# Layer 0 expert rows: latent rows normalised on TensorE and written plainly, context rows by accumulating DMA

## The chip, the cores and the metric

The kernel runs on one core of a Trainium2 chip. The metric is the device time of one execution in microseconds. Three executions of the kernel before took 1258.33, 1256.99 and 1256.77 us, with a median of 1256.99 us.

## The reference, cut to what matters

Two layers run over 256 latent tokens (x) and 256 context tokens (ctx), each row 1024 wide. After the mixer of a layer, every token row is normalised and modulated, and the 512 rows of layer 0 go through a mixture of 16 experts:

```python
m  = (silu(c) @ mod_w[l] + mod_b[l]).reshape(bsz, 1, 6, D)      # latent rows
mc = (silu(c_ctx) @ mod_w[l] + mod_b[l]).reshape(1, 1, 6, D)    # context rows
...
x = x + m[:, :, 2] * y
h = rms_norm(x, norm2_g[l]) * (1 + m[:, :, 4]) + m[:, :, 3]
if need_ctx:                                                    # layer 0 only
    xc = xc + mc[:, :, 2] * yc
    hc = rms_norm(xc, norm2_g[l]) * (1 + mc[:, :, 4]) + mc[:, :, 3]
    tokens = concatenate([h, hc])                               # 512 rows
    out = hierarchical_moe(tokens, router_g, router_e, w1, w3, w2)
```

With A2 = norm2_g * (1 + m4) and shift = m3, a row is h = rstd * (x * A2) + shift. The rstd is known only when the whole row of x is there; the shift is one row of 1024 numbers for all latent tokens and another for all context tokens. The experts pick their tokens by top-1 group and top-2 experts, so each expert needs a gather of rows of h.

## The kernel before, in words

All is written in one class, `Trunk`, for a scheduler that gives each engine one list of instructions and the semaphore waits between the lists; an engine works off its list in order. Work that may lie beside other work (modulation, shared norms, weight splitting) is written as generators that are woven into the main loops. SBUF is held by an allocator, `Arena` (`F.get`, `F.free`): a tile takes a free block, so what a write has to wait for depends on which block it was given and who used that block last. Weights come through `Stream` objects: `ws` holds loads of 1 MB each, all issued on the SP queue at L159, and `ws.add(F.fits(2048) - n)` gives it all the slots that still fit less a reserve. The reserve for the experts of a layer is the table `RES`.

The modulation rows are made half by half in `mod_half`: 8 k-steps of matmuls (L417), a bias add (L422, L424), a transpose, and four small DMAs on the ACT queue (L439) that write the rows to a DRAM tile `md[l, g]`. `mod_row` (L469) reads such a row back, broadcast over 128 partitions, also on the ACT queue.

`finish` closes the mixer. It loads A2 (`mod_row`), and while the output projection comes out piece by piece (L331 to L333, L550, L553) it makes x * A2 (L1300) into `H`, squares (L1329) and router logits (L1308 to L1323). In layer 0 it makes a DRAM tile `hd` of 512 rows and fills it with the shift rows by four broadcast DMAs from `md` (L1289), two of latent and two of context rows.

`moe` then computes rstd (ends in L298), and in layer 0 scales the four 128-row pieces of `H` by it on ScalarE (L1391) and adds each to `hd` with an accumulating DMA on the POOL queue (L1392). Beside this VectorE works the top-k and the ranks of the tokens (L1422 to L1479). At L1829 and L1835 every engine loads a flag and branches (whether an expert has overflowed). The experts follow: POOL gathers 128 rows of `hd` for each (L1483), TensorE transposes them (L1530), and ScalarE and VectorE split weights and rows for three-term products (L322, L325, L331 to L333, L1539, L1540).

Layer 1 has only latent rows; its rows for the experts don't pass through `hd`. There the same `finish` loads A2 (L469), which L1300 needs.

Of the kernel before, what the change touches and what calls it, by code (L numbers as in the profile page):

```python
# [8 lines left out]
F32 = mybir.dt.float32  # L9
F32R = mybir.dt.float32r  # L10
BF = mybir.dt.bfloat16
I32 = mybir.dt.int32
AF = mybir.ActivationFunctionType
OP = mybir.AluOpType
AX = mybir.AxisListType

P = 128
D = 1024
# [216 lines left out]
BQ = "sync"  # L235
HR = 4
HP = 0, 1, 0, 0
RES = 3, 3
FA = 2, 2
FB = 9, 9  # L240
NYY = 4
# [10 lines left out]
class Trunk:  # L252
# [146 lines left out]
    def mod_half(self, l, g, h):  # L399

        nc, I, F = self.nc, self.I, self.F
        ms, mb = F.get(256), F.get(256)

        def rows(dst, src):
            for i in range(src.shape[0]):
                nc.sync.dma_start(dst[32 * i:32 * i + 32], src[i:i + 1].to_broadcast([32, 256]))
        rows(mb, I["modb"][l, g, h])
        if g == 2:  # L410
            g2 = F.get(256)
            rows(g2[0:64], I["n2g"][l, h])
        acc = self.bank("m")
        for k in range(KC):
            raw = self.wm.take()
            for i in range(4):
                nc.tensor.matmul(acc[32 * i:32 * i + 32, 0:256], self.cs[:, k, :], raw[:, i * 256:(i + 1) * 256],  # L417
                                 start=(k == 0), stop=(k == KC - 1))
            self.wm.done(raw)
            if k < KC - 1:  # L420
                yield
        nc.vector.tensor_tensor(ms, acc[:, 0:256], mb, op=OP.add)  # L422
        if g == 2:
            nc.vector.scalar_tensor_tensor(ms[0:64], ms[0:64], 1.0, g2[0:64], op0=OP.add, op1=OP.mult)  # L424
            F.free(g2)
        F.free(mb)
        if g:
            yield

            tp, dst = self.bank(), (self.sh if g == 1 else self.a2)[l]  # L430
            for b in range(2):
                nc.tensor.transpose(tp[:, b * P:(b + 1) * P], ms[:, b * P:(b + 1) * P], self.ident)
            src = tp[:, 0:256].rearrange("p (b j q x) -> p j q b x", b=2, j=2, q=2)
            for s in range(2):
                nc.vector.tensor_copy(dst[:, s, 4 * h:4 * h + 4].rearrange("p (q b) -> p q b", q=2),
                                      src[:, 2 - g, :, :, s])
        if g:
            for i in range(4):
                nc.scalar.dma_start(self.md[l, g][:, h, i // 2, 256 * (i % 2):256 * (i % 2) + 256],  # L439
                                    ms[32 * i:32 * i + 2])  # L440
            F.free(ms)
        else:
            self.mr[l, h] = ms
        yield
# [811 lines left out]
    def finish(self, l, mix):  # L1256

        F, nc = self.F, self.nc
        ns = len(self.X)
        A2 = F.get(ns, D)  # L1260
        for s in range(ns):
            self.mod_row(A2[:, s], l, 4, s)

        rts, bR = F.get(ns, KC, 32), F.get(ns, 32)
        self.bR = bR
        for s in range(ns):
            nc.vector.tensor_tensor(rts[:, s], self.rt,
                                    self.a2[l][:, s].rearrange("p (k o) -> p k o", o=1).to_broadcast([P, KC, 32]), op=OP.mult)

        pr, pq = F.get(ns, KC, 32), F.get(ns, 32)  # L1270
        for s in range(ns):
            nc.gpsimd.tensor_tensor(pr[:, s], self.rt,
                                    self.sh[l][:, s].rearrange("p (k o) -> p k o", o=1).to_broadcast([P, KC, 32]), op=OP.mult)
            nc.vector.tensor_reduce(pq[:, s], pr[:, s].rearrange("p k c -> p c k"), AX.X, OP.add)
        ps = self.bank()
        nc.tensor.matmul(ps[:, 0:32 * ns], self.msk("ones"), pq.rearrange("p s c -> p (s c)"), start=True, stop=True)
        nc.scalar.copy(bR, ps[:, 0:32 * ns].rearrange("p (s c) -> p s c", s=ns))
        F.free(pr, pq)
        self.ss, junk = F.get(4, 2), F.get(512, dt=BF)

        hb = F.get(2, 3, D, dt=BF) if ns == 1 else None
        if ns == 2:

            H, self.hd = [F.get(2, D) for s in range(2)], self.dp.tile([4 * P, D], F32, name=f"hd{l}")
            for s in range(2):
                src = self.md[l, 1][s, :, 1].rearrange("(o h) c -> o h c", o=1)
                for i in range(2):
                    t = 2 * s + i
                    nc.scalar.dma_start(self.hd[t * P:(t + 1) * P, :].rearrange("p (h c) -> p h c", h=2),  # L1289
                                        src.to_broadcast([P, 2, 512]))  # L1290
        self.ws.add(F.fits(2048) - FA[l])

        lg, hfR = [self.bank("m"), self.bank("a")][0:ns], Ring(F, 2, 2, 256)
        hR = Ring(F, HR, 2, 256) if ns == 1 else None
        wait, kept = ([], [], [], []), {}

        def scaled(c, s):
            sl = slice(256 * c, 256 * c + 256)
            h = kept[c, s] = hR() if ns == 1 else H[s][:, :, sl]
            nc.vector.tensor_tensor(h, self.X[s][:, :, sl], A2[:, s, sl].rearrange("p (o c) -> p o c", o=1)  # L1300
                                    .to_broadcast([P, 2, 256]), op=OP.mult)

        def keep(c, s):
            sl, h = slice(256 * c, 256 * c + 256), kept.pop((c, s))
            if ns == 2:
                return
            for i in range(3):
                nc.scalar.copy(hb[:, :, i, sl], h)  # L1308
                if i < 2:
                    (nc.gpsimd if HP[c] else nc.vector).tensor_tensor(h, h, hb[:, :, i, sl], op=OP.subtract)  # L1310

        def logits(c, s):

            ps, hf = self.bank(), hfR()
            for kk in range(2):
                for i in range(2):
                    nc.tensor.transpose(ps[:, 256 * kk + i * P:256 * kk + (i + 1) * P],
                                        self.X[s][:, i, 256 * c + kk * P:256 * c + (kk + 1) * P], self.ident)
            nc.scalar.copy(hf, ps.rearrange("p (k t) -> p k t", k=2))
            for kk in range(2):  # L1320
                k = 2 * c + kk
                j = k % 4
                nc.tensor.matmul(lg[s][32 * j:32 * j + 32, 0:256], rts[:, s, k], hf[:, kk], start=(k < 4), stop=(k >= 4))  # L1323

        def squares(c, s):
            if c % 2:
                for i in range(2):
                    t = 2 * s + i
                    nc.scalar.activation(junk, self.X[s][:, i, 256 * c - 256:256 * c + 256], AF.Square,  # L1329
                                         accum_out=self.ss[:, t, c // 2:c // 2 + 1])  # L1330

        def last(c, s):
            for i, f in enumerate((scaled, squares, logits, keep)):
                wait[i].append((c, s))
                if len(wait[i]) > LAG[i] * ns:
                    f(*wait[i].pop(0))

        self.pool_share = 0
        run_all(self.out_half(l, 1, mix, ns, last))
        for i, f in enumerate((scaled, squares, logits, keep)):  # L1340
            for cs in wait[i]:
                f(*cs)
        F.free(*self.gates, junk, hfR, *([hR] if hR else []), rts, self.rt, A2)
        self.R.free(*mix)
        if ns == 2:
            self.xgR = Ring(F, 3, D)
            for x in self.xgR.bufs:
                nc.gpsimd.memset(x, 0.0)
        self.ws.add(max(0, F.fits(2048) - FB[l]))
        if l:  # L1350
            self.swap()
        for t in range(2 * ns):
            self.dbg(f"xm{l}_{t}", self.x(t))
        self.moe(l, H if ns == 2 else hb, lg)
# [14 lines left out]
    def moe(self, l, hd, lg):  # L1369
# [15 lines left out]
            stt(L[:, t], lp[:, 32 * t:32 * t + 32], rs[:, t:t + 1], self.bR[:, t // 2], op0=OP.mult, op1=OP.add)  # L1385
        if ns == 2:

            H, hd = hd, self.hd
            for t in range(nt):
                h = H[t // 2][:, t % 2]  # L1390
                nc.scalar.activation(h, h, AF.Copy, scale=rs[:, t:t + 1])  # L1391
                nc.gpsimd.dma_start(hd[t * P:(t + 1) * P, :], h, accum_op=OP.add)  # L1392
            F.free(*H)
        tmp = []

        def T(n):
# [511 lines left out]
    def run(self, stages):  # L1908
        nc, tc, I, F, R = self.nc, self.tc, self.I, self.F, self.R
        w, m = self.sources(stages)  # L1910
        self.ws, self.wm = Stream(nc, F, w, 2048), Stream(nc, F, m, 1024)
        self.md = {(l, g): self.dp.tile([2, 2, 2, 512], F32, name=f"md{l}{g}") for l in range(2) for g in (1, 2)}
        self.mr, self.sh, self.a2 = {}, [F.get(2, KC) for l in range(2)], [F.get(2, KC) for l in range(2)]
        self.rest = self.mods((1, 1), (1, 2)) if "l1" in stages else iter(())
# [135 lines left out]
```

## Time and profile before

| what | value |
|---|---|
| median of three executions | 1256.99 us |
| the profiled execution's own time | 1263.97 us |
| its span | 1262.2 us |
| mean granted TensorE clock | 0.951 |
| TensorE busy | 1109.3 us, 88% |
| VectorE busy | 806.6 us, 64% |
| ScalarE busy | 560.0 us, 44% |
| GpSimd busy | 340.6 us, 27% |
| bytes moved by DMA | 317.09 MB, mean 251 GB/s |

The profile is of one execution, 6.98 us longer than the median of the three. The busy shares are means over stages that have different limits: the experts of layer 0 run from about 376 to 700 us of the span, those of layer 1 from about 1000 us to the end. What follows reads the stages one by one, by waits and by windows.

### The profile page before, as it was taken

To read this page: it belongs to the slowest core of one execution; us is meant where nothing else is said; L and a number is where in the kernel's file an instruction comes from. 1 tells how busy PE (TensorE), PEld (TensorE's weight loads), DVE (VectorE), ACT (ScalarE), POOL (GpSimd) and SP (SyncE) were. 2 spreads that over 40 slices of the span, in tenths; PEclk is the share of its full clock that TensorE was granted. 3 is DMA by queue.
4 is the path that set the end of the run, shared out by engine and by line. 5 is a ranking of instruction groups with operands and counts; after the bars stand their busy time and mean duration, and the time that the engine had idled before them with its cause. 6 is when DMAs were issued, how large, how long until landed. Compare 5 with 4: busy or idle time off the path is not lost. (4 is left out here: it accounts for less than half of the span.)

```text
span 1262.2 us, 18733 instructions
## 1 busy us (share of the span) xinstructions
PE 1109.3 (88%) x7206; PEld 780.4 (62%) x7206; DVE 806.6 (64%) x1376; ACT 560.0 (44%) x893; POOL 340.6 (27%) x214
## 2 busy tenths in 40 slices
PE   3998899999919999999999779988998599999996
PEld 1656665666717777777777356655777365555553
DVE  3576836555639999999898646998387533333232
ACT  3355525333417787887886323343353311111111
POOL 1331422233213444444532211344423200000000
PEclk9998988899959999999999888999998899999999
DMA  9663568266386999999983154343476789999960
GB/s 355 215 207 124 172 191 278 71 239 242 114 238 241 352 353 346 364 362 358 356 312 118 71 143 179 117 134 107 149 273 249 282 315 422 424 423 424 416 277 35
DMA packets 74977, 317.09 MB, mean 251 GB/s; under 512 B 20074, under 2 KB 26314, under 8 KB 46080
## 3 DMA queue, kind: packets, MB, share of 16 engines
q1 hardware_dynamic: 54656, 294.10, 61.4%
q0 software_dynamic: 4896, 10.20, 3.6%
q10 hardware_dynamic: 15328, 11.50, 3.3%
q8 instruction: 60, 0.98, 0.3%
q14 instruction: 37, 0.30, 0.1%
HBM read 310.74 MB, written 14.76 MB: 258 GB/s over the span
## 5 line engine op out<-in xcount | busy, mean ns | idle before, releaser
L322 ACT CAST arena_rw<-arena_f 128x1024 fp32r<-128x1024 f32 x256 | 265.1, 1050 | 177.7 <-PE b L333 111.3
L325 DVE TENSOR_TENSOR arena_rw<-arena_f,arena_rw 128x1024 fp32r<-128x1024 f32 x198 | 260.4, 1357 | 81.5 <-ACT arena_rw L322 80.9
L331 PE MATMUL b<-arena_rw,arena_rr 128*128 128x512 f32 (+1 forms) x736 | 275.1, 375 | 2.7 <-ACT arena_rr L1214 1.2
L332 PE MATMUL b<-arena_rw,arena_rr 128*128 128x512 f32 (+1 forms) x736 | 272.0, 370 | 0.0
L333 PE MATMUL b<-arena_rw,arena_rr 128*128 128x512 f32 (+1 forms) x736 | 270.1, 369 | 0.5 <-DVE arena_rr L1215 0.5
L325 POOL TENSOR_TENSOR arena_rw<-arena_f,arena_rw 128x1024 fp32r<-128x1024 f32 x58 | 144.4, 2490 | 235.8 <-ACT arena_rw L322 220.6
L331 PEld LDWEIGHTS b<-arena_rw,arena_rr 128*128 128x128 f32 x736 | 140.5, 191 | 37.9 <-issue 10.6
L333 PEld LDWEIGHTS b<-arena_rw,arena_rr 128*128 128x128 f32 x736 | 140.0, 191 | 25.6 <-issue 3.3
L332 PEld LDWEIGHTS b<-arena_rw,arena_rr 128*128 128x128 f32 x736 | 140.7, 191 | 21.2 <-issue 1.3
L417 PE MATMUL b<-arena_f,cs 128*32 128x256 f32 x768 | 70.2, 420 | 22.2 <-DMA arena_f<-in_modw 22.0
L331 PE MATMUL b<-arena_rr,arena_rw 128*128 128x512 f32 (+1 forms) x192 | 74.4, 391 | 2.7 <-ACT arena_rw L322 1.4
L1728 PE MATMUL b<-arena_f 128*64 128x256 f32 x656 | 76.0, 381 | 0.0
L333 PE MATMUL b<-arena_rr,arena_rw 128*128 128x512 f32 (+1 forms) x192 | 72.3, 380 | 4.1 <-DVE arena_rw L325 4.1
L332 PE MATMUL b<-arena_rr,arena_rw 128*128 128x512 f32 (+1 forms) x192 | 73.6, 384 | 1.0 <-POOL arena_rr L507 1.0
L1728 PEld LDWEIGHTS b<-arena_f 128*64 128x64 f32 x656 | 46.5, 137 | 24.2 <-issue 2.3
L417 PEld LDWEIGHTS b<-arena_f,cs 128*32 128x32 f32 x768 | 20.8, 113 | 56.3 <-issue 26.8
L1761 ACT CAST arena_rr<-arena_f 64x512 fp32r<-64x512 f32 x32 | 19.8, 618 | 69.7 <-DVE arena_f L1758 69.3
L1733 ACT ACTIVATE arena_f<-b 128x256 f32<-128x256 f32 x16 | 6.2, 385 | 98.0 <-PE b L1728 98.0
L331 PEld LDWEIGHTS b<-arena_rr,arena_rw 128*128 128x128 f32 x192 | 36.7, 192 | 18.2 <-issue 7.4
L1744 DVE COPY arena_f<-b 128x256 f32<-128x256 f32 x16 | 6.8, 424 | 64.1 <-PE b L1742 64.0
L1488 POOL DMA_INDIRECT yd<-arena_f x14 | 33.5, 2390 | 50.5 <-ACT arena_f L1578 50.5
L553 POOL TENSOR_TENSOR arena_f<-arena_f 128x512 f32<-128x512 f32 x21 | 30.5, 1458 | 57.1 <-DVE arena_f L550 54.8
(386 smaller groups left out, 1798.2 us busy)
## 6 DMA issues: line engine op xcount, KB each, us to landing
arena_f<-in_moe SPq DMA_DIRECT2D x192, 1024.0 KB
arena_f<-in_modw SPq DMA_DIRECT2D x96, 512.0 KB
arena_f<-in_wod SPq DMA_DIRECT2D x18, 1024.0 KB
arena_f<-in_wev SPq DMA_DIRECT2D x14, 1024.0 KB
arena_f<-md ACTq DMA_DIRECT2D x8, 512.0 KB
arena_f<-in_tok SPq DMA_DIRECT2D x4, 512.0 KB
yd<-arena_f SPq DMA_DIRECT2D x4, 512.0 KB
hd<-md ACTq DMA_DIRECT2D x4, 512.0 KB
```

The lines of the kernel that those rows point to most:

```text
L322: nc.scalar.copy(h, raw)
L325: eng.tensor_tensor(l, raw, h.bitcast(F32), op=OP.subtract)
L331: nc.tensor.matmul(ps, ah, bh, start=first, stop=False)
L332: nc.tensor.matmul(ps, ah, bl, start=False, stop=False)
L333: nc.tensor.matmul(ps, al, bh, start=False, stop=last)
L417: nc.tensor.matmul(acc[32 * i:32 * i + 32, 0:256], self.cs[:, k, :], raw[:, i * 256:(i + 1) * 256], start=(k == 0), stop=(k == KC - 1))
L553: (nc.vector if last and c == 3 else nc.gpsimd).tensor_tensor(xs, xs, tmp, op=OP.add)
L1488: self.nc.gpsimd.indirect_dma_start(out=yd[:, :], out_offset=bass.IndirectOffsetOnAxis(ap=dst, axis=0), in_=y, in_offset=None, bounds_chec ...
L1728: nc.tensor.matmul(p[64 * c:64 * c + 64, 256 * w:256 * w + 256], x[:, 4 * b + k], raw[:, 512 * k + 256 * c:512 * k + 256 * c + 256], start ...
L1733: nc.scalar.activation(u, p[:, 0:256], AF.Tanh, scale=0.5)
L1744: nc.vector.tensor_copy(ut, ps[:, 0:256].rearrange("p (b c) -> p b c", b=2))
L1761: nc.scalar.copy(yh[r, c], y[r])
```

## The change

In `mod_half` the first two modulation rows of the second group of layer 0 (the shift rows) are also split into three bf16 parts, which four small DMAs on the ACT queue write to a new DRAM tile `mb2`. In `finish` of layer 0, `hd` gets its broadcast fill for the context rows only; the three parts of the latent shift are loaded into a small tile `S3` of 3 partitions. In `moe` the two context pieces are scaled on ScalarE and added to `hd` by POOL's accumulating DMA, as before. For the two latent pieces TensorE multiplies a diagonal matrix of the rstd (`dgR`, made by ScalarE) by x * A2, and a second matmul with ones over 3 partitions adds the shift parts in the same PSUM bank; ScalarE copies the bank back to `H`, and the SP queue writes the rows to `hd` with a plain DMA. The reserve of weight slots for layer 0 goes from 3 to 2.

```diff
-RES = 3, 3
+RES = 2, 3
@@ mod_half
+            if (l, g) == (0, 1):
+                pt = F.get(3, 256, dt=BF)
+                for i in range(3):
+                    nc.vector.tensor_copy(pt[64:, i], ms[64:])
+                    if i < 2:
+                        nc.vector.tensor_tensor(ms[64:], ms[64:], pt[64:, i], op=OP.subtract)
+                for q in range(2):
+                    nc.scalar.dma_start(self.mb2[:, :, h, 256 * q:256 * q + 256], pt[64 + 32 * q:66 + 32 * q])
+                F.free(pt)
@@ finish
-            for s in range(2):
-                src = self.md[l, 1][s, :, 1].rearrange("(o h) c -> o h c", o=1)
-                for i in range(2):
-                    t = 2 * s + i
-                    nc.scalar.dma_start(self.hd[t * P:(t + 1) * P, :].rearrange("p (h c) -> p h c", h=2),
-                                        src.to_broadcast([P, 2, 512]))
+            self.S3 = F.get(D, dt=BF)
+            nc.scalar.dma_start(self.S3[0:3], self.mb2[0].rearrange("i h c -> i (h c)"))
+            src = self.md[l, 1][1, :, 1].rearrange("(o h) c -> o h c", o=1)
+            for t in range(2, 4):
+                nc.scalar.dma_start(self.hd[t * P:(t + 1) * P, :].rearrange("p (h c) -> p h c", h=2),
+                                    src.to_broadcast([P, 2, 512]))
@@ moe
-            H, hd = hd, self.hd
-            for t in range(nt):
-                h = H[t // 2][:, t % 2]
-                nc.scalar.activation(h, h, AF.Copy, scale=rs[:, t:t + 1])
-                nc.gpsimd.dma_start(hd[t * P:(t + 1) * P, :], h, accum_op=OP.add)
-            F.free(*H)
+            H, hd, dgR = hd, self.hd, F.get(2, P)
+            for t in range(2):
+                nc.scalar.activation(dgR[:, t], self.ident, AF.Copy, scale=rs[:, t:t + 1])
+            for t in range(2):
+                h, g = H[0][:, t], H[1][:, t]
+                nc.scalar.activation(g, g, AF.Copy, scale=rs[:, 2 + t:3 + t])
+                nc.gpsimd.dma_start(hd[(2 + t) * P:(3 + t) * P, :], g, accum_op=OP.add)
+                for c in range(2):
+                    sl, ps = slice(512 * c, 512 * c + 512), self.bank("a")
+                    nc.tensor.matmul(ps, dgR[:, t], h[:, sl], start=True, stop=False)
+                    nc.tensor.matmul(ps, self.oneb[0:3], self.S3[0:3, sl], start=False, stop=True)
+                    nc.scalar.copy(h[:, sl], ps)
+                nc.sync.dma_start(hd[t * P:(t + 1) * P, :], h)
+            F.free(*H, self.S3, dgR)
@@ allocation at the start
+        self.mb2 = self.dp.tile([2, 3, 2, 512], BF, name="mb2")
```

New lines stand at other numbers: L1391 and L1392 become L1404 and L1405, L469 becomes L479, L1483 becomes L1502, L1835 becomes L1854, L1300 becomes L1310. The new ones are L445 and L447 (parts on VectorE), L449 (their DMAs), L1401 (diagonal), L1408 and L1409 (the two matmuls), L1410 (copy) and L1411 (plain write).

ScalarE at the start of the experts of layer 0, before; L1391 scales a piece of `H`, L1422 and L1427 are exponentials of the routing, L469 loads a gate row:

```order
L1391 ACTIVATE arena_f<-arena_f 128x1024 [waits DMAHW3_49,DVE_49]
L1391 ACTIVATE arena_f<-arena_f 128x1024 [waits DMAHW4_49]
L1391 ACTIVATE arena_f<-arena_f 128x1024 x2
L1422 ACTIVATE arena_f<-arena_f 128x16 [waits DVE_49,Activation_49]
L1427 ACTIVATE arena_f<-arena_f 128x4 [waits DVE_49]
L469 DMA arena_f<-md_73 128x2x512 [waits DMAHW7_49,DVE_49,Activation_49]
L1829 TENSOR_LOAD arena_f [waits DMAHW1_49,DVE_49]
```

The same place of ScalarE in the changed kernel (L1441 and L1446 are the two exponentials):

```order
L1401 ACTIVATE arena_f<-mskt,arena_f 128x128 [waits DMAHW6_49,DVE_49,Activation_49]
L1401 ACTIVATE arena_f<-mskt,arena_f 128x128
L1404 ACTIVATE arena_f<-arena_f 128x1024
L1410 COPY arena_f<-b_2550 128x512 [waits PE_49]
L1404 ACTIVATE arena_f<-arena_f 128x1024
L1410 COPY arena_f<-b_2554 128x512 [waits PE_49]
L1441 ACTIVATE arena_f<-arena_f 128x16 [waits DMAHW4_49,DVE_49]
L1410 COPY arena_f<-b_2561 128x512 [waits PE_49]
L1446 ACTIVATE arena_f<-arena_f 128x4 [waits DVE_49]
L1410 COPY arena_f<-b_2565 128x512 [waits DMAHW7_49,PE_49]
```

Two scalings are replaced by four copies that wait for TensorE, the exponentials now stand between these copies, and the gate row's load has moved behind the branch.

SP and POOL at the same place in the changed kernel; first SP, where L1411 writes latent rows to `hd` (before, the row ahead of TENSOR_LOAD was another weight load, and no weight load stood between TENSOR_LOAD and the branch):

```order
L159 DMA arena_f<-in_moe 128x2048 [waits DMAHW5_49,DMAHW0_49,DVE_49]
L1411 DMA hd_2203<-arena_f 128x1024 [waits DMAHW1_49,Activation_49]
L1411 DMA hd_2203<-arena_f 128x1024 [waits DMAHW2_49,Activation_49]
L1848 TENSOR_LOAD arena_f [waits DMAHW6_49,DVE_49]
L1848 ISA x2
L159 DMA arena_f<-in_moe 128x2048 [waits DMAHW2_49,DMAHW3_49,DMAHW1_49,DVE_49]
L1854 COMPARE_AND_BRANCH
```

Then POOL, where the first gather stands ahead of the branch (before, it stood behind it and behind four accumulating DMAs):

```order
L1405 DMA hd_2203<-arena_f 128x1024 [waits DMAHW2_49,DVE_49,Activation_49]
L1405 DMA hd_2203<-arena_f 128x1024 [waits Activation_49]
L1502 DMA arena_f<-hd_2203,arena_f 128x1024 [waits DMASW1_49,DMAHW1_49,DMASW0_49,DMAHW2_49,DVE_49,Pool_49]
L1848 TENSOR_LOAD arena_f [waits DMAHW6_49,DVE_49]
L1854 COMPARE_AND_BRANCH
```

The gather now waits for two semaphores of POOL's own queue and two of the hardware queues, and SP holds a weight load in front of its branch that waits for hardware DMAs.

ScalarE's queue in layer 1, around the load of A2, before; `md_75` is the modulation row, L439 writes it, L469 loads it, L1214 copies transposed rows of the mixer's output out of PSUM:

```order
L439 DMA md_75<-arena_f 2x256 [waits DMAHW4_49]
L322 CAST arena_rw<-arena_f 128x1024 [waits PE_49]
L322 CAST arena_rw<-arena_f_6980 128x1024 [waits DMAHW6_49,PE_49]
L322 CAST arena_rw<-arena_f_6980 128x1024 [waits PE_49]
L1214 ACTIVATE arena_rr_6976<-b_7333,cst 128x128 [waits PE_49]
L1214 ACTIVATE arena_rr_6976<-b_7346,cst 128x128 [waits PE_49]
L1277 COPY arena_f<-b_7363 128x32 [waits PE_49]
L1214 ACTIVATE arena_rr_6976<-b_7333,cst 128x128 [waits DVE_49]
L469 DMA arena_f<-md_75 128x2x512 [waits DMAHW4_49,DMAHW3_49,DMAHW7_49,DMAHW0_49,Pool_49]
```

The same place in the changed kernel:

```order
L439 DMA md_76<-arena_f 2x256 [waits DMAHW1_49]
L322 CAST arena_rw<-arena_f 128x1024 [waits PE_49]
L479 DMA arena_f<-md_76 128x2x512 [waits DMAHW3_49,DMAHW6_49,DMAHW1_49,DMAHW0_49]
L322 CAST arena_rw<-arena_f_7010 128x1024 [waits PE_49] x2
L1224 ACTIVATE arena_rr_7006<-b_7363,cst 128x128 [waits PE_49]
L1224 ACTIVATE arena_rr_7006<-b_7376,cst 128x128 [waits PE_49]
L1287 COPY arena_f<-b_7393 128x32 [waits PE_49]
```

The load of A2 stands six rows earlier and no longer waits for POOL; the block of SBUF that it fills is another one.

## Rows read from the trace of the kernel before

**Rows 1.** Experts' windows: length, busy PE PEld DVE ACT POOL, PEclk, DMA share, GB/s

```profile
450.00:500.00 50.00, 47.17 (x242) 38.15 (x242) 47.25 (x49) 39.96 (x48) 25.14 (x11) 1.00 0.96 355
...
1080.00:1130.00 50.00, 48.36 (x533) 29.69 (x533) 18.42 (x33) 10.32 (x26) 0.00 (x0) 1.00 1.01 423
```

**Rows 2.** Windows just before layer 0's experts, same columns

```profile
359.00:362.00 3.00, 0.00 (x0) 0.00 (x0) 0.51 (x1) 0.00 (x0) 0.00 (x0) 0.50 1.08 244
...
371.00:374.00 3.00, 0.00 (x0) 0.00 (x0) 0.00 (x0) 0.00 (x0) 0.00 (x0) 0.50 1.01 411
```

**Rows 3.** Timeline of TensorE from 372 us: start, length, line, idle before

```profile
375.72 1.94 PE L1530 MATMUL b<-mskt,arena_f 128*128 128x128 f32 x8 [18.91 <-DMA arena_f<-hd,arena_f]
```

**Rows 4.** Timeline of POOL from 346 us

```profile
349.17 2.93 POOL L1392 DMA_DIRECT2D hd<-arena_f  x3 [14.84 <-ACT arena_f L1391]
352.26 0.87 POOL L1392 DMA_DIRECT2D hd<-arena_f  x1 [0.16 <-ACT arena_f L1427]
366.72 1.11 POOL L1483 DMA_INDIRECT arena_f<-hd,arena_f  x1 [13.60 <-DMA hd<-arena_f]
```

**Rows 5.** Timeline of SP's queue from 362 to 372 us

```profile
366.18 1.42 SPq L159 DMA_DIRECT2D arena_f<-in_moe  x3
```

**Rows 6.** Line L1392: us from issue to landing

```profile
DMA to landing us min/median/max: 5.6/10.1/13.5
```

**Rows 7.** Windows at the end of layer 1's mixer

```profile
960.00:970.00 10.00, 8.56 (x53) 8.57 (x54) 9.69 (x22) 2.25 (x3) 3.62 (x2) 0.66 0.50 191
...
980.00:990.00 10.00, 3.81 (x33) 3.61 (x31) 1.79 (x3) 0.62 (x1) 1.51 (x2) 0.86 0.86 344
990.00:1000.00 10.00, 6.89 (x38) 4.91 (x39) 5.68 (x9) 6.80 (x16) 5.52 (x4) 0.62 0.19 56
```

**Rows 8.** Waits from 950 to 1010 us: total us, times, longest us

```profile
PE b L1323 <- ACT arena_f L1319: 9.3, 1, 9.3
DVE arena_f L1300 <- DMA arena_f<-md: 8.5, 1, 8.5
...
DVE arena_f L550 <- DMA arena_f<-md: 1.4, 1, 1.4
```

**Rows 9.** Chain that ended last, from 940 us: start, length, what

```profile
949.88 7.81 DMA arena_f<-md
...
970.49 4.47 POOL arena_f L553 x2
974.98 13.05 DMA arena_f<-md
988.12 0.69 DVE arena_f L1300
```

**Rows 10.** Windows in the early part of layer 0

```profile
140.00:150.00 10.00, 10.00 (x68) 7.17 (x60) 10.00 (x10) 2.70 (x5) 7.43 (x4) 1.00 0.66 206
...
200.00:210.00 10.00, 6.91 (x53) 3.21 (x52) 9.68 (x15) 6.48 (x13) 2.90 (x2) 0.95 0.94 338
210.00:220.00 10.00, 10.00 (x34) 4.30 (x32) 6.84 (x19) 4.41 (x13) 2.08 (x2) 0.50 0.88 288
```

**Rows 11.** Timeline of ScalarE from 346 us

```profile
347.69 4.27 ACT L1391 ACTIVATE arena_f<-arena_f 128x1024 f32<-128x1024 f32 x4 [1.00 <-DVE arena_f L298]
```

**Rows 12.** Groups by line and shape: busy us, mean ns, idle before

```profile
L1319 ACT COPY arena_f<-b 128x512 f32<-128x512 f32 x12 | 6.7, 582 | 1.4 <-PE b L1317 1.0 <-PE b L1323 0.3
```

**Rows 13.** Timeline of TensorE in layer 0's attention, at full and at half clock

```profile
202.80 1.98 PE L739 MATMUL b<-arena_f 64*128 64x512 f32 x4
...
213.76 3.78 PE L739 MATMUL b<-arena_f 64*128 64x512 f32 x4
```

**Rows 14.** Timeline of ScalarE's queue from 945 us

```profile
959.43 2.58 ACTq L439 DMA_DIRECT2D md<-arena_f  x4
```

**Rows 15.** Timeline of VectorE: one operation of 64 x 256

```profile
960.97 0.41 DVE L424 SCALAR_TENSOR_TENSOR arena_f<-arena_f 64x256 f32<-64x256 f32 x1
```

## The prediction

> **What bounds the kernel now.** I read the windows first, stage by stage. In the experts of both layers TensorE is the bound: 47.17 us of 50 in layer 0 (VectorE 47.25 beside it) and 48.36 of 50 in layer 1, both at full clock [rows 1]. What arrives earlier at such a stage leaves it earlier by as much, unless the weight stream holds it. So the change must be read where TensorE stands still, and two such places touch it.
>
> The first is ahead of layer 0's experts. The windows show TensorE without work and at half clock (0.50), while the DMA engines are full [rows 2]. The timelines, read backwards, give the chain: TensorE's first transposes start at 375.72 after 18.91 us of waiting for the gathered rows [rows 3]; POOL issued that gather at 366.72 after waiting 13.60 us for `hd` [rows 4]; `hd` was late through the four accumulating DMAs, issued from 349.17 to 353.13 [rows 4], which took 5.6 us (least) to 13.5 us (most) to land [rows 6]. The first landing is then 349.17 + 5.6 = 354.8, the last 353.13 + 13.5 = 366.6: (366.6 - 354.8) / 3 = 3.9 us per accumulate, one behind another. The gather and three weight loads that start at 366.18 [rows 5] share the engines, and the rows land 9.0 us after the issue.
>
> The second is the end of layer 1's mixer. The waits show VectorE at L1300 8.5 us behind a DMA from `md`, and TensorE 9.3 us behind what follows it [rows 8]; the window 980 to 990 has TensorE busy 3.81 of 10 [rows 7]. The chain gives the reason: POOL's two L553 end at 974.96, only then A2's load is issued, and it lands 13.05 us later [rows 9]. Its wait for POOL is one for a block of SBUF; the modulation rows that it reads were written from 959.43 to 962.01 [rows 14].
>
> **The change part by part.** *Layer 0, rows for the experts.* The path starts where rstd is there, at 347.69 [rows 11]. Two scalings of 4.27 / 4 = 1.07 us go, two small diagonal makings (between nothing and the 0.58 us of a 128x512 copy [rows 12]; I take 0.3) and four copies of 0.58 come: ScalarE works 2 x 0.3 + 2 x 1.07 + 4 x 0.58 = 5.1 us for 4.27. In the new order the first context piece is scaled by 349.4 and the second, behind one copy, by 351.0. POOL issued 0.4 us after the scale's end before (349.17 against 347.69 + 1.07), so the two accumulates go out at about 349.8 and 351.4. The first lands 5.6 us later, at 355.4, and the second 3.9 behind it, at 359.3.
>
> TensorE's part: L739 shows two f32 matmuls of 512 columns in 1.98 us at full clock and 3.78 at half [rows 13], so 0.99 or 1.89 each; four of them, with four one-pass matmuls that I bound by 0 and half of that, make 4.0 to 5.9 us at full clock and 7.6 to 11.3 at half. The work begins at 348.1, when the clock is still up, so I take about 5, and the last copy ends near 353.5 (at half clock up to 360). The two plain writes leave SP at about 351.8 and 353.6. They hold 2 x 0.524 MB, at 411 GB/s [rows 2] 2.6 us of all engines, half of which I put in front of the second accumulate: `hd` stands at 360.6, against 366.7. Bounds: the second accumulate cannot land before 351.4 + 5.6 = 357.0, that is -9.7; with both writes and the weight load that SP now holds ahead of its branch in front (2.55 us for 1.05 MB, and a second load behind it), it is 359.3 + 2.6 + 5.1 = 367.0, that is +0.3.
>
> The row shows accumulates that hold the engines at a share of 1.08 with 244 GB/s of all traffic [rows 2]: they use the engines, not one queue. The Trainium skill (DMA: Bandwidth & Descriptors, Rules for kernel authors) says that spreading transfers over SP, ACT and GpSimd gives no bandwidth, as all run on the same 16 engines and interleave; this trace agrees by that full share. By the rule the gain would only be the engine time that a plain write saves against an accumulate, 2 x (3.9 - 1.3) = 5.2 us, and if the weight loads move in between, none; by the issue times above it is 6.1.
>
> The gather keeps its 9.0 us; its wait is now two semaphores more, and POOL's branch is queued behind it, with the second gather behind that, which no engine needs sooner than the first. TensorE starts at 369.6: **-6** for this term. The two exponentials stand behind copies by about 1 us; the routing on VectorE that needs them was done before 360 (0.51 us of work in 359 to 362 [rows 2]), ahead of `hd`, so this costs nothing, and 1 us if `hd` comes at its lower bound.
>
> *Layer 1, load of A2.* With another block it stands behind L439 and one L322 and waits for the written rows alone. I put its issue at 964 to 966, in a window where the DMA share is 0.50 [rows 7]. With the 7.81 us of the earlier gate load it lands at 973, with its present 13.05 at 979; VectorE reaches L1300 at 988.12 - 8.49 = 979.6 [rows 9]. So the 8.5 us go whole; what is late next is POOL's L553 and TensorE's pieces, which share the work with VectorE. At most TensorE's 9.3 is won, at least nothing. I take **-8**. The gate load ahead of it also moves up, and VectorE's 1.4 us [rows 8] may go; I count half, **-0.7**.
>
> *Early part.* The shift parts are 5 operations per half at no more than 0.41 us [rows 15], 2.05 us; one half falls where VectorE is full (10.00 of 10 from 140 to 150 [rows 10]), so 0 to +2; the other half beside its idle time. Two broadcasts of 0.52 MB fewer and another order of attention matmuls act on 200 to 210, where TensorE works 6.91 of 10 and then falls to half clock [rows 10]: that can give up to 3.1 us of idle, and the half-clock stretch is priced as a rival. I take **+0.7** in all. The four 2-row DMAs to `mb2` and the load of `S3` lie beside attention; without that cover they cost ScalarE's queue five issues of 0.65 us (2.58 / 4 [rows 14]), 3 us. RES lets one more weight slot in, at nothing.
>
> *Sum.* -6 - 8 - 0.7 + 0.7 = -14. The profiled execution took 1263.97 us (span 1262.2), 6.98 above the median; with the same distance it is 1250 against 1264, and 1257 - 14 = **1243** for the median of runs. The term of layer 0 passes through layer 0's experts since they are bound by TensorE and VectorE at a DMA share of 0.96 [rows 1].
>
> **The rivals.** *Same engines, no earlier `hd`.* The writes and the released weight loads fill what the accumulates leave, and the gather starts at 366 or later. For it: the share of 1.08; against it: a plain write moves its bytes once. Then only layer 1 counts: 1257 - 8 = 1249.
>
> *Layer 1's gain is taken back by the weight stream.* Layer 1's experts run at a DMA share of 1.01 and 423 GB/s beside TensorE's 48.36 of 50 [rows 1], so either could set the end. If the stream does, the 8 us and the 0.7 stay as a wait in the experts, only the -6 of layer 0 has a chance to stay, since it moves the stream's start too, and 1257 - 6 = 1251 is left. Against it: the DMA share of 0.19 from 990 to 1000 [rows 7] says that the slots were full before the experts began, so the stream moves with TensorE.
>
> *The clock stays up after 210.* If TensorE no longer waits in 200 to 210, the work of 210 to 230 runs at 1.98 for 3.78 [rows 13]: 20 us become 10.5. Then -14 - 9 = 1234. Against it: the waits there are for modulation weights, which the change doesn't load sooner.
>
> *Slower: weights of layer 0's experts come late.* Place: SP's queue. Two writes of `hd` that wait for ScalarE, and a weight load that waits for these writes to land, now stand ahead of SP's branch, and the pool of slots is cut otherwise. The experts run at a DMA share of 0.96 [rows 1], so a slot that comes free later is felt in each of 16. From 14 / 16 = 0.9 us per expert it eats the whole gain; at 1.5 us it is 1257 - 14 + 24 = 1267, at 1.2 us 1262. Against it: 355 GB/s is well below the 423 of layer 1, so there is room to catch up.
>
> **How the numbers follow.** The forecast, both terms (1237 to 1250): 0.50. Same engines (1249): 0.13. Gain taken back (1251): 0.10. Clock (1234): 0.08. Late weights (1258 to 1267): 0.11. Several small losses that cancel it (1254.5 to 1259.5): 0.08. What a measurement of this kernel can't tell from no change is 0.2%, 2.5 us. Faster: 0.50 + 0.13 + 0.10 + 0.08 less 0.03 for a taken-back gain that ends within 2.5 us: 0.78; same 0.08 + 0.03 = 0.11; slower 0.11. The range 1236 to 1257 leaves out most of the clock case, half of the cancelled one and the late weights, about 0.2; it holds the lower bounds of both big terms (1257 - 9.7 - 9.3 = 1238) and the upper one of either.
>
> **What would show it.** In the changed profile: the first expert transposes start near 369 (in that execution's own time from rstd: 22 us after it for 28); two accumulates, the second landing about 8 us after its issue; two writes of `hd` on SP at 4 us after rstd; A2's load in layer 1 ahead of the transposed copies, and no wait of VectorE at L1310 for it; the experts' windows at 47 and 48 of 50 as before. The prediction is wrong if the gather is issued 19 us after rstd as before, if TensorE's busy share in the experts falls, or if the 8.5 us at A2 return as another wait in 960 to 1010.

## The result

The changed kernel takes 1242.47 us (median of 4, from 1239.62 to 1245.43); the kernel before takes 1257.66 us (median of 4, from 1256.77 to 1264.73). The ratio is 0.9867, with a 95% interval of 0.9821 to 0.9914, so the change saves 15 to 17 us. The forecast was 1243, from 1236 to 1257. The profiled execution of the changed kernel took 1244.74 us (span 1242.8), 19.4 us of span less than the one before.

What follows compares the two profiles between points that both have: the last step of rstd on VectorE (L298), the issue of the first gather, the first transposes of the experts, the first matmul that sums layer 0's experts at their end (L1657), the first L1149 in layer 1's mixer, the first matmul of the sums of layer 1's experts (L1684) and the end. A2 is loaded and used between L1149 and L1684.

| stretch | forecast | before | after | difference |
|---|---|---|---|---|
| start to rstd (L298) | +0.7 | 347.50 | 346.14 | -1.4 |
| rstd to the first gather's issue | -6.1 | 19.22 | 14.20 | -5.0 |
| gather's issue to the first transposes | 0 | 9.00 | 6.17 | -2.8 |
| layer 0's experts, to L1657 (now L1676) | 0 | 310.1 | 310.2 | +0.1 |
| from there to L1149 (now L1159) in layer 1 | 0 | 249.6 | 249.8 | +0.2 |
| L1149 to L1684 (now L1703), with A2 | -8.7 | 62.6 | 52.1 | -10.5 |
| L1684 to the end | 0 | 264.2 | 264.2 | 0.0 |

The layer 0 place first, in the changed kernel: timelines of ScalarE, POOL, SP and TensorE, with the idle time before a row in brackets. L1401 makes the diagonals, L1404 scales, L1410 copies out of PSUM, L1405 accumulates, L1411 writes to `hd`; these rows answer to [rows 3, 4, 5, 11].

```profile
346.38 0.69 ACT L1401 ACTIVATE arena_f<-mskt,arena_f 128x128 f32<-128x128 f32 x2 [1.05 <-DVE arena_f L298]
346.98 1.13 ACT L1404 ACTIVATE arena_f<-arena_f 128x1024 f32<-128x1024 f32 x1
...
352.02 0.59 ACT L1410 COPY arena_f<-b 128x512 f32<-128x512 f32 x1 [0.91 <-PE b L1409]
...
355.60 0.59 ACT L1410 COPY arena_f<-b 128x512 f32<-128x512 f32 x1 [0.68 <-PE b L1409]
```

```profile
348.44 1.08 POOL L1405 DMA_DIRECT2D hd<-arena_f  x1 [15.46 <-ACT arena_f L1404]
351.42 0.91 POOL L1405 DMA_DIRECT2D hd<-arena_f  x1 [1.90 <-ACT arena_f L1404]
360.34 1.10 POOL L1502 DMA_INDIRECT arena_f<-hd,arena_f  x1 [8.00 <-DVE arena_f L1498]
```

```profile
352.63 3.90 SPq L1411 DMA_DIRECT2D hd<-arena_f  x2
359.59 6.59 SPq L159 DMA_DIRECT2D arena_f<-in_moe  x3
```

```profile
346.84 2.07 PE L1408 MATMUL b<-arena_f 128*128 128x512 f32 x2 [0.82 <-ACT arena_f L1401]
...
351.92 1.96 PE L1408 MATMUL b<-arena_f 128*128 128x512 f32 x2
...
354.12 1.13 PE L1408 MATMUL b<-arena_f 128*128 128x512 f32 x2
...
366.51 1.94 PE L1549 MATMUL b<-mskt,arena_f 128*128 128x128 f32 x8 [7.33 <-DMA arena_f<-hd,arena_f]
```

Both accumulates now land 5.5 us after their issue (5.5 and 5.6; before 5.6 to 13.5 [rows 6]). TensorE's first three pieces run at half clock (1.96 to 2.08 us each), so the last copy ends at 356.2 and the last write leaves then. The profile names VectorE's L1498 as what the gather waited for; that row ended at 360.0. But one weight load had gone out at 359.59, and that load waits for the same plain writes of `hd`, so these had landed by then. The other profiles decide between the two. In seven profiles, those of the changed kernel and of all its variants below but the last, the last load that waits for a write goes out 0.74 to 0.83 us before the gather. The end of the same L1498 row moves meanwhile from 3.36 us before the gather (the run without TensorE, below) to 0.01 us after it (the run with loads beside the gather). So the landing of the last write releases the gather.

The windows of the same place (columns as in [rows 2]) show the DMA engines full for 9 us, from 350 to 359. Before, traffic began at about the same time, the engines were full until 363, and they were in part busy until the gather at 366.7. These are the windows of the changed kernel:

```profile
347.00:350.00 3.00, 3.00 (x4) 0.94 (x5) 2.62 (x15) 1.63 (x4) 1.08 (x1) 0.50 0.00 0
350.00:353.00 3.00, 3.00 (x5) 0.60 (x3) 0.77 (x7) 1.82 (x4) 0.91 (x1) 0.50 1.14 180
353.00:356.00 3.00, 3.00 (x20) 0.89 (x18) 1.51 (x11) 1.09 (x3) 0.00 (x0) 0.90 0.95 157
356.00:359.00 3.00, 0.54 (x16) 0.49 (x16) 2.60 (x12) 0.18 (x1) 0.00 (x0) 0.67 0.93 362
359.00:362.00 3.00, 0.18 (x7) 0.10 (x4) 1.69 (x5) 0.00 (x0) 1.10 (x1) 0.50 0.45 115
```

Which queue held the engines is in the profiles too (q0 is POOL's queue, q1 SP's, q10 ScalarE's; then packets, MB, share of the 16 engines). First the kernel before, from 350 to 366.7, with the row of ScalarE's queue behind it, then the changed kernel, from 350 to 359.6:

```profile
q0 software_dynamic: 576, 2.10, 72.4%
q10 hardware_dynamic: 487, 0.96, 17.2%
```

```profile
353.97 10.61 ACTq L469 DMA_DIRECT2D arena_f<-md  x2
```

```profile
q0 software_dynamic: 288, 1.05, 67.6%
q1 hardware_dynamic: 288, 1.05, 26.9%
```

The share times the length of the stretch gives the time for which a queue held all the engines. Four accumulates held them for 12.1 us, 3.0 each; in the changed kernel two hold them for 6.5 us, 3.2 each, and the two plain writes for 2.6 us, 1.3 each. So two writes in place of two accumulates save 3.0 us of the engines. Before, another 2.9 us went to the two gate rows that ScalarE's queue loaded (L469), from 358 on; in the changed kernel these loads go out from 365.18 on (L479), after the gather. No run moved the gate rows alone.

In layer 1 the load of A2 goes out at 952.80, right after the rows it reads, and VectorE's first L1310 (L1300 before) waits 1.47 us for POOL and not for the load, for which it waited 8.5 us before [rows 8]. First ScalarE's queue, then VectorE:

```profile
947.41 3.29 ACTq L439 DMA_DIRECT2D md<-arena_f  x4
...
952.80 0.39 ACTq L479 DMA_DIRECT2D arena_f<-md  x1
```

```profile
968.94 0.69 DVE L1310 TENSOR_TENSOR arena_f<-arena_f 128x512 f32<-128x512 f32 x1 [1.47 <-POOL arena_f L563]
```

### The profile page after: what moved, and what is told of

It is laid out like the page before. It is cut to its first block, busy times and chain, and to the rows that moved or that the text cites. A ratio compares the mean times of both kernels' runs of the same rounds, so it can differ in the third digit from the quotient of the medians.

```text
span 1242.8 us, 18783 instructions
## 1 busy us (share of the span) xinstructions
PE 1110.9 (89%) x7218; PEld 777.8 (63%) x7218; DVE 811.3 (65%) x1386; ACT 560.6 (45%) x897; POOL 339.1 (27%) x212
## 5 line engine op out<-in xcount | busy, mean ns | idle before, releaser
L325 DVE TENSOR_TENSOR arena_rw<-arena_f,arena_rw 128x1024 fp32r<-128x1024 f32 x198 | 255.9, 1333 | 76.6 <-ACT arena_rw L322 76.3
L325 POOL TENSOR_TENSOR arena_rw<-arena_f,arena_rw 128x1024 fp32r<-128x1024 f32 x58 | 144.6, 2493 | 223.5 <-ACT arena_rw L322 206.5
L417 PE MATMUL b<-arena_f,cs 128*32 128x256 f32 x768 | 69.3, 417 | 20.4 <-DVE arena_f L492 13.4
L331 PEld LDWEIGHTS b<-arena_rr,arena_rw 128*128 128x128 f32 x192 | 37.1, 194 | 18.3 <-issue 7.4
L333 PEld LDWEIGHTS b<-arena_rr,arena_rw 128*128 128x128 f32 x192 | 37.0, 193 | 12.8 <-DVE arena_rw L325 4.3
```

Source lines behind the costliest of these rows:

```text
L325: eng.tensor_tensor(l, raw, h.bitcast(F32), op=OP.subtract)
L331: nc.tensor.matmul(ps, ah, bh, start=first, stop=False)
L333: nc.tensor.matmul(ps, al, bh, start=False, stop=last)
```

## The experiments

The times of one program spread more than the first runs told: 29 runs of the kernel before, beside the first four experiments, lie between 1250.46 and 1266.36 us. So the 95% intervals count where a kernel ran several times, and a kernel that ran once is read by its profile.

**Layer 1 alone.** The kernel before with another block for A2:

```diff
+        skip = [F.get(D) for _ in range(1)] if ns == 1 else []
         A2 = F.get(ns, D)
+        F.free(*skip)
```

> The kernel before with one edit: in layer 1 A2 is given another free block of SBUF, so that its load no longer waits for POOL. Theory (the block is a gain of its own, 7.9 us between the two profiles): the wait of VectorE at L1300 (8.5 us) falls below 1.5 us, the start of layer 0's experts stays at 375 to 377 us of the span, and the time falls by 6 to 9 us against before. Rival (layer 1's experts are bound by their weight stream, the earlier start comes back as waits for in_moe): the wait at L1300 goes, but the time falls by less than 2 us.

Ratio 0.9952 (0.9916 to 0.9989), or -6 us (-1.4 to -10.6). In the profile the load goes out at 962.90 for 974.98, the first transposes stay at 375.7, and TensorE works 8.43 of 10 us in 980 to 990 for 3.81 [rows 7]:

```profile
980.00:990.00 10.00, 8.43 (x43) 5.68 (x43) 7.03 (x12) 8.55 (x20) 4.67 (x3) 0.83 0.44 157
```

VectorE's wait there is at most 1.47 us, for POOL. The span is 8.9 us shorter. The block is a gain of its own; how large is less sure. The interval reaches just into the under 2 us of the rival, and in this profile the last stretch, from L1684 to the end, took 267.2 us for 264.2, so up to 3 us of the gain may have come back there.

**Layer 1 taken away again.** The changed kernel with POOL put in front of the load:

```diff
         A2 = F.get(ns, D)
+        if ns == 1:
+            nc.gpsimd.tensor_copy(A2[:, 0, 0:8], self.X[0][:, 1, 768:776])
```

> The changed kernel with one edit: a copy of 8 columns on POOL into A2's block, behind the L563 of the mixer's first half, puts the load of A2 in layer 1 back where it stood before, behind POOL. Theory: the gain against before shrinks by the 8 us of layer 1, to 6 to 9 us, and VectorE waits 7 to 9 us for the load again. Rival (the gain of layer 1 comes from weights or from the gate load that moved up): VectorE waits again but the time stays within 3 us of the changed kernel's.

1249.77 us, ratio 0.9932 (0.9901 to 0.9962) where the changed kernel has 0.9867: 0.0065, or 8 us, of the gain are gone (1 to 15 us with both intervals). The stretch from L1149 to L1684 takes 59.5 us for the changed kernel's 52.1, and the chain of waits has the old picture back:

```profile
960.40 4.46 POOL arena_f L563 x2
965.14 11.12 DMA arena_f<-md
```

VectorE waits 6.1 us for the load, a little under the 7 to 9 expected. With the run before, from both sides, 6 to 8 us of the change are the place of one tile in SBUF, each with an uncertainty of several us.

**The shift parts alone.** The kernel before plus the part of the diff in `mod_half`, with `mb2` read by nobody.

> The kernel before plus the shift parts alone: 10 operations on VectorE and 4 small DMAs to DRAM, whose result nobody reads; four broadcasts and four accumulating DMAs stay. Theory (the parts cost VectorE time where it is full, and only the rest of the change gives time back): rstd before layer 0's experts comes 1 to 5 us later than at 347.5 us, and the kernel is 1 to 5 us slower than before. Rival (the early part is a trade of clock stretches, the parts themselves are hidden): rstd within 1 us of 347.5, the time the same.

Ratio 1.0075 (1.0045 to 1.0104), 5.6 to 13 us slower: more than the theory allows. The profile does not show that much. TensorE's wait for L688 grows to 9.4 us from 6.7, but rstd is at 347.98, and its span is 0.5 us under that of before. VectorE's rows say why the parts are dear where they are: the same subtraction took 0.42 us at best and 2.50 in the first half, and one cast in the second half (L445) took 5.21 where the others took 0.29, beside POOL's L722 from 185.91 to 191.53. The ten operations add up to 13.4 us.

```profile
142.57 1.41 DVE L447 TENSOR_TENSOR arena_f<-arena_f 64x256 f32<-64x256 f32 x1
...
146.82 2.50 DVE L447 TENSOR_TENSOR arena_f<-arena_f 64x256 f32<-64x256 f32 x1
...
186.48 5.21 DVE L445 CAST arena_f<-arena_f 64x256 bf16<-64x256 f32 x1
```

A second profile of this kernel and one of the kernel before followed.

> The kernel before plus the shift parts alone, once more, for a second profile. The first profile put rstd at 347.98 us against 347.50, the times were 9 us longer. Theory (the profile fell on a favourable stretch of the clock): rstd 3 to 9 us later than 347.5 this time. Rival (the loss lies behind rstd): rstd within 1.5 us of 347.5 and a longer stretch further on.

> The kernel before, unchanged, for a second profile: shows which stretches vary between executions of one program. Expected: layer 0's gap from rstd to the first transposes within 1 us of 28.2 us, the wait at A2's load in layer 1 within 2 us of 8.5, the stretches at half clock near 150 to 235 us within 4 us.

They put rstd at 349.05 with the parts and at 345.87 without (1263.58 and 1261.88 us for these executions). The 349.05 is 1.55 us later than 347.5, between the theory and the rival. Over both pairs the parts delay rstd by 1.8 us on average. The other stretches of the kernel before held within the bounds but for one: its gap from rstd to the transposes was 29.5 us, 1.3 more. Some 7 us of the nine stand in no profile. The clock that each execution was granted says where to look: its mean is 0.947 over the 12 executions with the parts and 0.954 over the 29 of the kernel before beside them; of those 29 the shortest (1250.46 us) had 0.964 and one of the longest (1266.05 us) 0.947. The two profiled executions of the kernel before had 0.951 and 0.949, against 0.948 and 0.950 with the parts, and were themselves 7.0 and 5.7 us over its medians. So they were slow ones of their kernel, and a loss that lies in the clock hardly shows between these profiles. Why the clock is lower with the parts there is not shown.

**The reserve.** The changed kernel with `RES = 3, 3` as before the change.

> The changed kernel with the reserve of weight slots at 3, 3 as before instead of 2, 3. Theory (the reserve is only there to make room and has no part in the gain): within 2.5 us of the changed kernel, the first transposes of layer 0's experts 19 to 21 us after rstd. Rival (the shorter gather comes from the one more slot, whose load was there earlier): the gather takes about 9 us again and 3 us of the gain go.

1243.24 us, ratio 0.9886 (0.9840 to 0.9932); transposes 20.2 us after rstd, gather 6.1 us. No part of the reserve in the gain is seen.

**The parts made small.** The changed kernel, with the parts taken out of `mod_half` and made in `finish`:

```diff
+            sq, pt = F.get(8), F.get(3, 8, dt=BF)
+            for h in range(2):
+                nc.scalar.dma_start(sq[64 * h:64 * h + 64], self.md[l, 1][0, h, 1].rearrange("(q k) -> q k", k=8))
+            for i in range(3):
+                nc.vector.tensor_copy(pt[:, i], sq)
+                if i < 2:
+                    nc.vector.tensor_tensor(sq, sq, pt[:, i], op=OP.subtract)
+            nc.scalar.dma_start(self.mb2.rearrange("i (p k) -> p i k", k=8), pt)
+            nc.scalar.dma_start(self.S3[0:3], self.mb2)
```

> The changed kernel with the shift parts made elsewhere: instead of ten operations on 64x256 in mod_half, the shift row is read back from md as 128 partitions x 8 in finish and split there by five operations on 128x8, written to mb2 by one DMA. Theory (the parts' cost on VectorE near 150 us is real and stays in the changed kernel's time): TensorE's wait for L688 goes from 9.4 back to 7 us or less, rstd comes 1 to 5 us earlier than at 346.1 us, and the time falls by 2 to 8 us against the changed kernel, to 1235 to 1241. Rival (in the whole kernel the early delay is given back by the clock further on, as the profiles say): rstd within 1 us of 346.1, time within 2 us of 1242.5.

1238.67 us, ratio 0.9879 (0.9850 to 0.9909). In the profile rstd comes at 341.21, 4.9 us earlier than in the changed kernel, and TensorE's wait is back at 6.9 us. One profile alone says little here: rstd lies between 343.05 and 348.40 in the six profiles of the changed kernel and of its variants that keep the parts in `mod_half`. With small parts it is 341.21 here and 339.43 in the last experiment, ahead of all six. After 200 the granted clock is higher than before the change (0.83 and 1.00 in these windows for 0.73 and 0.68):

```profile
200.00:220.00 20.00, 16.94 (x88) 7.18 (x81) 19.98 (x44) 11.39 (x28) 7.04 (x6) 0.83 0.78 267
220.00:240.00 20.00, 20.00 (x136) 13.25 (x138) 12.37 (x33) 8.80 (x23) 4.82 (x5) 1.00 0.20 67
```

So by these profiles the early part of the changed kernel holds two things of about 5 and 6 us that nearly cancel: the parts, and a half-clock stretch after 209 that got shorter with half of the broadcasts gone and the matmuls in another order (which of these two did it was not tried apart). The ratios of this kernel and of the changed one overlap, so that it is faster is shown in the profile only.

**The last write.** The changed kernel with one write for each 512 columns:

```diff
                     nc.scalar.copy(h[:, sl], ps)
-                nc.sync.dma_start(hd[t * P:(t + 1) * P, :], h)
+                    nc.sync.dma_start(hd[t * P:(t + 1) * P, sl], h[:, sl])
```

> The changed kernel with each latent row block written to hd by two DMAs of 512 columns, each issued after its own copy, instead of one of 1024 columns after both. Theory (the gather waits for the last write, whose issue hangs on TensorE's last piece): the last write holds half the bytes, the gather goes out 0.5 to 1.5 us earlier than 14.2 us after rstd, the time falls by about 1 us, which is within the noise. Rival (the gather waits for VectorE's one-hot rows, L1498, as the profile names it): the gather's issue stays at 14.2 us after rstd.

The gather went out 15.0 us after rstd for 14.2, ratio 0.9925 (0.9895 to 0.9955): no gain; neither bound of the theory held.

**No TensorE.** The changed kernel with the latent rows scaled on ScalarE and the latent shift left out:

```diff
-                for c in range(2):
-                    ...
-                    nc.scalar.copy(h[:, sl], ps)
+                nc.scalar.activation(h, h, AF.Copy, scale=rs[:, t:t + 1])
```

> The changed kernel with the latent rows scaled on ScalarE and written plainly; the latent shift is left out of the rows for the experts (no matmul, no copy). Theory (TensorE at half clock makes the last write late): the gather goes out 2 to 4 us earlier, 10 to 12 us after rstd, then held by the second accumulate and by the routing. Rival (the accumulates hold it already): the gather stays at 14 us after rstd.

In its one execution all four transfers are issued by 349.3, yet the gather goes out 14.06 us after rstd: the theory was wrong. The windows (same columns) tell why:

```profile
348.00:350.00 2.00, 0.54 (x14) 0.45 (x14) 1.63 (x11) 1.12 (x3) 0.91 (x1) 0.50 1.07 221
...
354.00:356.00 2.00, 0.00 (x0) 0.00 (x0) 0.71 (x2) 0.00 (x0) 0.00 (x0) 0.50 1.01 274
356.00:358.00 2.00, 0.00 (x0) 0.00 (x0) 0.51 (x1) 0.00 (x0) 0.12 (x1) 0.50 0.10 29
```

The engines are full from 347.6 to 356.2, 8.6 us, for the same two accumulates and two writes that take 9 us when TensorE staggers them. So what TensorE does in the changed kernel lies beside the transfers and costs nothing. By queue, from 347 to 357, the accumulates hold the engines for 5.7 us and the writes for 3.1.

**The first gather.** Two runs on why it takes 6.2 us and no more 9.0. The kernel before with `RES = 6, 3`:

> The kernel before with the reserve at 6, 3 instead of 3, 3: three weight slots fewer in layer 0, so that no three weight loads start together with the first gather. Theory (the first gather took 9.0 us because three weight loads of 1 MB ran beside it, and 6.2 us in the changed kernel because they had gone ahead): the rows arrive 5 to 7 us after the gather's issue, hd lands as late as before (19 us after rstd). Rival (the gather takes 9 us by itself where it is issued behind accumulates): 8 to 9.5 us.

It missed its aim: three weight loads started with the gather all the same (364.02 to 365.96, gather 364.49), as they came from slots that were queued on SP behind the load that waits for `hd`. The gather took 7.7 us, between theory and rival, and went out 18.4 us after rstd. Layer 1 moved as well, though only the reserve of layer 0 was changed: A2's load went out at 960.90 for 974.98, and the stretch from L1149 to L1684 took 55.6 us for 62.6. So loads were put beside the gather in the changed kernel instead:

```diff
+            for i in range(2):
+                nc.sync.dma_start(H[i].rearrange("p a b -> p (a b)"), self.I["moe"][0, 15, i])
             F.free(*H, self.S3, dgR)
```

> The changed kernel with two more loads of 1 MB on SP, into H's two blocks, which start when the last write and accumulate of hd have landed and which nobody reads: the traffic that stood beside the first gather before. Theory (the first gather was 9.0 us before and 6.2 us in the changed kernel because of the weight loads beside it): the rows arrive 8 to 11 us after the first gather's issue, the gather's own issue stays 14 us after rstd. Rival (the gather is shorter for another reason, such as fewer accumulates ahead of it on POOL's queue): 5.5 to 7 us.

```profile
356.90 1.59 POOL L1504 DMA_INDIRECT arena_f<-hd,arena_f  x1 [8.71 <-DVE arena_f L1539]
```

```profile
365.05 2.15 PE L1551 MATMUL b<-mskt,arena_f 128*128 128x128 f32 x9 [8.96 <-DMA arena_f<-hd,arena_f]
```

The rows land 8.2 us after the issue: 2 us more than in the changed kernel, with 2 MB of loads beside it, so the neighbours lengthen the gather. Two loads bring back 2.0 of the 2.8 us between 9.0 and 6.2. In the changed kernel only one of the three loads goes out before the gather, the other two after 365.

**H kept out of the stream.** The small split, with `F.free(*H, ...)` behind the dealing of slots and `RES = 1, 3`.

> The changed kernel with the small split of the shift (five operations on 128x8) and with H's blocks freed only after the weight slots are dealt out (reserve 1, 3), so that no weight load waits for hd. Theory (SP's queue is held by a load that waits for hd, and what starts then runs beside the gather): with H's blocks out of the stream the loads behind the branch go out before the gather or long after it, the gather takes 5 to 6 us, and the time stays within 3 us of the small split's 1238.7. Rival (a slot fewer starves layer 0's experts): the experts' windows fall below 46 of 50 us of TensorE and the time rises by over 3 us.

1240.83 us, ratio 0.9869 (0.9831 to 0.9906). The experts are not starved (48.13 of 50 us in 450 to 500), but the scheduler put POOL's branch ahead of the first gather, which goes out 17.2 us after rstd and takes 8.6 us beside two loads: the gap was 25.8 us, and only the early rstd (339.43) kept the time level. The time stayed within the theory's 3 us, but the gather of 5 to 6 us did not come, and nothing is won.

## Why the prediction was right

The sum held: -14 forecast, -15.2 by the medians, -19.4 between the two profiles, of which the one before lay 6.3 us above the median of 1257.66 and the other 2.3 above that of 1242.47. It did not hold term by term. Against the profiles the terms were off by 1.1 us one way (`hd`) and by 2.8, 1.8 and 2.1 the other (gather, A2, early part), and that so little of this shows in the medians is luck.

- *Layer 0, `hd` earlier by 6.1:* measured 5.0. That the transfers' hold on the engines sets the time was right, and so was 1.3 us for a write. The 3.9 us for an accumulate was not: it was taken from their landings, and from 358 on a gate row's load shared the engines with them. In the row with the share of 1.08, read as the accumulates' own, that load has 0.26. An accumulate held the engines for 3.0 to 3.2 us, so the trade itself saves about 3.0. Up to 2.9 more can come from the gate rows, which left this stretch and had no term in the sum. The sum by the rule that all queues share the 16 engines gave 5.2 (the Trainium skill, DMA: Bandwidth & Descriptors, Rules for kernel authors); the run without TensorE agrees with the rule, with 8.6 us of full engines for 9. That 5.2 is so near the 5.0 is luck, as it stands on the 3.9; with 3.0 it would be 3.4. The rival built on that rule was too strict: no weight load filled the gap, because the load that SP now holds ahead of its branch waits for `hd` and left only at 359.59.
- *TensorE at about 5 us for its part:* measured 8.7 us, from 346.84 to 355.6, as the granted clock was 0.50 (1.2 GHz) from 347 to 353. It cost nothing, as the run without TensorE shows (gather 14.06 us after rstd for 14.20). That was luck and not seen: the last copy ended at 356.2, not 353.5, and the second accumulate landed only at 356.9.
- *The gather keeps its 9.0:* wrong by 2.8 us, the largest error of the sum; 2.0 of it are shown by the run with loads beside the gather. The row with three loads at 366.18 was in the prediction, but not the step from it, that loads which leave at other times free the gather.
- *Passing through layer 0's experts:* right, 310.1 and 310.2 us.
- *A2 in layer 1, -8 and -0.7:* 10.5 between the profiles, 6 to 8 by the times of the two runs that moved it alone. The issue was forecast at 964 to 966 of the old time; 952.80 with 8.9 us of earlier gain is 961.7. Between these two profiles the weight stream took nothing back: L1684 to the end is 264.2 us in both.
- *Early part, +0.7:* -1.4, by two effects that the profiles put at 5 and 6 us, and that the prediction had priced at +2 at most and as a rival with a chance of 0.08. The price of 0.41 us per operation came from one row of VectorE; in the changed kernel the ten took 9.7 us where that price gives 4.1, the dearest 2.50.
- *Late weights, slower (a rival):* did not come; TensorE worked 48.13 of 50 us in 450 to 500.

Not shown: what lowers the clock in the plain executions of the kernel with the parts alone, how much of the 5.0 us at `hd` comes from the gate rows, and what shortened the half-clock stretch after 209.

## What to carry to other kernels

Count an accumulating DMA by the time it holds the shared engines, not by its queue: 512 KB took 3.0 to 3.2 us of all of them here, a plain write 1.3, and moving half of the bytes to plain writes paid although the arithmetic behind them ran at half clock. Price such a transfer by its own queue's share, since landings also hold what other queues move meanwhile (here the gate rows). Before crediting a change, look for what it shifts in the allocator: some half of this gain came from a tile in another layer that no longer waited for POOL, and two lines would have had it without the rest. And time new work on an engine where it will run, not at its best row.

## What the hardware showed

A subtraction of 64x256 on VectorE took 0.42 us in one place and 2.50 in another. The long one ran from 146.8 to 149.3 in the run with the parts alone, and its twin in the changed kernel from 147.66 to 150.16, while POOL's L325 ran from 147.04 to 149.88:

```profile
147.04 2.84 POOL L325 TENSOR_TENSOR arena_rw<-arena_f,arena_rw 128x1024 fp32r<-128x1024 f32 x1
```

The Trainium skill (SBUF — State Buffer, SBUF: two separate sides) says that a VectorE instruction with two inputs from SBUF and a GpSimd instruction that reads SBUF need the same pair of ports, which the one that starts first holds for its whole instruction while the other is blocked. These rows agree, as the subtraction ends 0.28 us after POOL's row; no run here tried it apart. The first traffic of an accumulate appears at 350, 1.6 us after its issue at 348.44, with a DMA share of 0.00 between.
